# Layer 1 of a two-layer streaming trunk: attention steps and memory turns at fixed product counts inside each main block

## The chip, the cores and the metric

The kernel runs on one core of a Trainium2 chip. The metric is device time in microseconds (us) of one execution. Before the change the median is 1432.3 us of 3 runs (1431.83 to 1434.07).

## What is computed

The program is one inference step of an encoder trunk with two layers, for a prompt of 512 tokens and a sample of 32, which are carried side by side as 544 columns. Layer 0 is a recurrent mixer and is not touched here. Layer 1, cut to what matters:

```python
def diff_layer(x, mk, mv, k_past, v_past, ..., w_out, w_in, ...):
    h = rmsnorm(x, norm_w)
    q, k, v, qm, gate = split(h @ w_in)      # 12 heads of 128 columns each in q, k, v; 4 memory heads in qm; 16 gate blocks
    # per head, q and k have two halves (maps) of 64; blocks of 128 queries, keys masked by chunks of 64
    attn = softmax(q1 @ k1.T / 8) - lam * softmax(q2 @ k2.T / 8)
    o = rmsnorm(attn @ v, subln) * (1 - lam_init)
    y_mem = softmax(qm @ mk.T * 128 ** -0.5) @ mv      # 256 memory rows
    out = concatenate([o, y_mem]) * silu(gate)
    return x + out @ w_out, k, v
```

The prompt's attention is causal by chunks over its own 512 keys; the 32 sample tokens see 128 cached keys and their own 32. Keys and values of both are outputs too.

## The kernel before

Every engine is called through the helper class `Queue`, so line 104 stands at nearly every instruction of the profile; the tiles' names tell them apart. Engines are TensorE (PE, with its weight loads as PEld), VectorE (DVE), ScalarE (ACT), GpSimd (POOL) and SyncE (SP), which issues DMAs.

**Main blocks.** Products of the projection are taken in 32 bits by splitting: a block of 1024 x 128 weights, loaded as two halves `raw`, is split into `whi` (a cast on ACT, two per block) and `wlo` (a subtraction on DVE, two per block); the activations are held as `hh` and `hl`. For each of two column halves of 272 and each of 8 slices of 128 rows, PE does `whi` x `hh`, `whi` x `hl` and `wlo` x `hh` into one bank `ps_g`: 48 products to a block. `proj` and `gemm` (or `steps`, a generator with a stop after each product) emit them, and an evacuation function takes each half out of the bank (`k`, `v`, `qp`/`qs`, the gate `sg`, or the memory query `mq`). `used()` then emits the split of the next block and the load of a later one, in the order of the list from `blocks1`. `whi` and `wlo` have 2 buffers, `raw` 5.

**Banks.** PSUM has 3 banks for `ps_g` (pool `psg`, also `ps_mo`), 2 in `psm` (turnings: `ps_kv`, `ps_kvs`, `ps_ckT`, `ps_aT`, `ps_oT`; memory scores `ps_mm`), 1 in `psx` (`ps_o`, `ps_os`) and 2 in `psc` (scores `ps_s`, and `ps_sc`).

**Layer 1** runs 3 groups of 4 heads. For each head `diff_group` emits the K block, the split of the keys into `kh` and `kz` (with DMAs that fill the other half of `kh`), the Q block, the V block, and then the whole attention of the head in one piece: keys and values turned (`kt`, `vt`, also written out), the sample's keys and values (`vs`), the sample's scores `ps_sc` copied to `ssb`, and for each of four blocks `t` of 128 queries: two maps of scores `ps_s` of (t + 1) x 128 columns, two passes each; mask by memset; maximum `snm` (DVE), exponential `pt` (ACT); `combine` (DVE); t + 1 transposes into `ps_aT`, copied to `aT` (ACT); t + 1 passes of `ps_o`, copied to `ot` (DVE) and squared (`jk`, ACT). After four heads the sample's output (`ps_saT`, `ps_os`, `ps_osT`), the scaling of `ot`, its transposes `ps_oT` and four gate blocks follow. Groups 0 and 1 then have two memory heads each (`mem_head`): a query block and a gate block, with the steps of `mem_steps` emitted behind them. That makes 56 main blocks, and then the output product.

**What sets the order.** In layer 1 the flag `ordered` is off, so a scheduler places each engine's instructions at build time, from the order in which they are emitted, the data they need and the buffers that come free. It may slide a piece of attention between products that are emitted later. At run time each engine's queue is fixed.

## Time and profile before

| | before |
|---|---|
| median of 3 runs | 1432.3 us |
| profiled execution, its own time | 1432.36 us |
| its span in the profile | 1430.4 us |
| PE busy | 1391.5 us (97%) |
| PEld busy | 1309.5 us (92%) |
| DVE, ACT, POOL busy | 64%, 58%, 26% |
| main products `ps_g` of layers 0 and 1, each of three kinds | 1808 |

The span is what the trace covers of the profiled execution; the difference to its own time lies around it. A busy share is an average over stages with different limits. Matmuls are pipelined and overlap, so the busy time of PE includes time in which one of them stands behind another. Weight loads are the second view of the same queue: each matmul has one.

### The profile page before, as it was taken

The numbers are of one execution on the slowest core, as the hardware profiler recorded it, in microseconds if no ns is written. First come the engines' busy times: TensorE is split into PE (matmuls) and PEld (weight loads), VectorE is DVE, ScalarE is ACT, GpSimd is POOL, SyncE is SP. The second block draws the span as 40 slices with busy tenths as digits, with TensorE's granted clock in tenths as the row PEclk, the third lists the DMA queues.
The fourth block names the chain that finished last, engine by engine and source line by source line (L and its number), as shares of the span: only waits on it lengthen the run. The fifth ranks groups of instructions, "written<-read, shape, count | busy, mean of one in ns | idle before, by whom it ended". The sixth has DMA issues, their size and how long they took to land.

```text
span 1430.4 us, 31910 instructions
## 1 busy us (share of the span) xinstructions
PE 1391.5 (97%) x11877; PEld 1309.5 (92%) x11877; DVE 917.7 (64%) x2345; ACT 828.8 (58%) x2282; POOL 375.0 (26%) x838
## 2 busy tenths in 40 slices
PE   8999999999999999999999999999999999999997
PEld 6998899999999998988999999989999989999997
DVE  5776678778777778566734656574465746557443
ACT  5766677777777676656433456554566446565222
POOL 2046557655686557600000220000000001000100
PEclk9999999999999999999999999999999999999999
DMA  7533222333223322432644562323333223332321
GB/s 225 157 106 80 60 58 75 80 83 75 73 66 82 97 68 55 122 93 79 192 142 128 148 188 81 91 79 89 97 90 85 83 75 95 90 103 62 97 80 71
DMA packets 264036, 139.45 MB, mean 97 GB/s; under 512 B 57721, under 2 KB 252802, under 8 KB 263882
## 3 DMA queue, kind: packets, MB, share of 16 engines
q1 hardware_dynamic: 263818, 137.41, 34.1%
q8 instruction: 94, 1.54, 0.5%
q14 instruction: 60, 0.49, 0.1%
q10 hardware_dynamic: 64, 0.02, 0.0%
HBM read 111.12 MB, written 22.91 MB: 94 GB/s over the span
## 4 chain that ended last, share of the span: by engine, by line
PE 82%; DVE 8%; ACT 6%; issue 2%; DMA 1%; SPq 1%; DVEq 0%; ACTq 0%
PE ps_g L104 57%; PE ps_c L104 4%; PE ps_s L104 2%; PE ps_o L104 2%; PE ps_at L104 2%; DVE wlo L104 1%; PE ps_v L104 1%; PE ps_mo L104 1%; PE ps_mm L104 1%; PE ps_aT L104 1%; SPq L104 1%; PE ps_yc L104 1%; PE ps_ss L104 1%; ACT whi L104 1%; PE ps_w L104 1%
## 5 line engine op out<-in xcount | busy, mean ns | idle before, releaser
L104 PE MATMUL ps_g<-hh,wlo 128*128 128x272 f32 x1808 | 538.4, 299 | 2.5 <-DVE wlo L104 2.5
L104 PE MATMUL ps_g<-hh,whi 128*128 128x272 f32 x1808 | 538.6, 299 | 0.2 <-DVE memk L104 0.2
L104 PE MATMUL ps_g<-hl,whi 128*128 128x272 f32 x1808 | 531.8, 295 | 0.6 <-DVE hl L104 0.3
L104 PEld LDWEIGHTS ps_g<-hh,wlo 128*128 128x128 f32 x1808 | 341.7, 189 | 7.5 <-DVE wlo L104 3.6
L104 PEld LDWEIGHTS ps_g<-hh,whi 128*128 128x128 f32 x1808 | 342.4, 190 | 5.2 <-issue 0.5
L104 PEld LDWEIGHTS ps_g<-hl,whi 128*128 128x128 f32 x1808 | 341.8, 189 | 5.0 <-DVE hl L104 1.3
L104 DVE TENSOR_TENSOR wlo<-raw,whi 128x512 fp32r<-128x512 f32 x314 | 216.8, 703 | 191.6 <-ACT whi L104 187.8
L104 ACT CAST whi<-raw 128x512 fp32r<-128x512 f32 x314 | 189.9, 617 | 172.0 <-PE ps_g L104 99.0
L851 POOL TENSOR_TENSOR tm<-u,m 102x84 f32<-102x84 f32 (+23 forms) x341 | 146.6, 430 | 163.2 <-DMA m<-sc 137.4
L853 POOL TENSOR_TENSOR u<-u,tm 102x84 f32<-102x84 f32 (+23 forms) x341 | 147.8, 434 | 26.7
L104 PE MATMUL ps_g<-hi,whi 128*128 128x272 f32 x512 | 148.9, 291 | 0.0
L104 PE MATMUL ps_g<-hi,wlo 128*128 128x272 f32 x512 | 147.8, 289 | 0.8 <-DVE wlo L104 0.8
L104 PE MATMUL ps_g<-lo,whi 128*128 128x272 f32 x512 | 147.6, 288 | 0.0
L1312 POOL TENSOR_TENSOR lo<-og,hi 128x544 fp32r<-128x544 f32 x8 | 13.7, 1708 | 484.0 <-DVE og L104 348.8
L104 PEld LDWEIGHTS ps_g<-hi,wlo 128*128 128x128 f32 x512 | 96.4, 188 | 1.0 <-DVE wlo L104 1.0
L104 PEld LDWEIGHTS ps_g<-lo,whi 128*128 128x128 f32 x512 | 96.4, 188 | 0.0
L104 PEld LDWEIGHTS ps_g<-hi,whi 128*128 128x128 f32 x512 | 96.4, 188 | 0.0
L104 DVE SCALAR_TENSOR_TENSOR SB<-ps_c,dl,sd 64x64 f32<-64x64 f32 x168 | 47.5, 283 | 43.9 <-PE ps_c L104 40.5
L1731 POOL TENSOR_TENSOR hl<-hn,hh 128x544 fp32r<-128x544 f32 x8 | 12.7, 1588 | 212.9 <-ACT hh L104 212.7
L104 ACT COPY sv<-ps_c 64x64 f32<-64x64 f32 x192 | 39.3, 205 | 44.5 <-PE ps_c L104 42.7
L104 ACT ACTIVATE sg<-ps_g 128x272 f32<-128x272 f32 x64 | 25.3, 395 | 64.0 <-PE ps_g L104 62.2
L104 ACT ACTIVATE pt<-ps_s,snm 128x128 f32<-128x128 f32 (+3 forms) x96 | 50.7, 529 | 17.9 <-DVE snm L104 16.9
(388 smaller groups left out, 2599.6 us busy)
## 6 DMA issues: line engine op xcount, KB each, us to landing
raw<-in_rw_in_dram SPq DMA_DIRECT2D x114, 256.0 KB
raw<-in_df_in_dram SPq DMA_DIRECT2D x112, 256.0 KB
raw<-in_w_out_dram SPq DMA_DIRECT2D x64, 256.0 KB
oscr<-sg SPq DMA_DIRECT2D x16, 272.0 KB
lo<-oscr SPq DMA_DIRECT2D x16, 272.0 KB
m<-sc SPq DMA_DIRECT2D x33, 128.0 KB
raw<-in_w_mem_v_dram SPq DMA_DIRECT2D x16, 256.0 KB
kh<-kh SPq DMA_DIRECT2D x24, 136.0 KB
```

The source lines that it names most:

```text
L104: return lambda *a, **k: self.trunk.tie(self, issue(*a, **k))
L851: nc.gpsimd.tensor_tensor(tm[:, :n, :wd], u3[:, :n, kx : kx + 1].to_broadcast(sh), m3[:, kx : kx + 1, kx + 1 :].to_broadcast(sh), ALU.mult)
L853: nc.gpsimd.tensor_tensor(u3[:, :n, kx + 1 :], u3[:, :n, kx + 1 :], tm[:, :n, :wd], ALU.add)
L1312: (self.nc.gpsimd if g % 2 and self.o1 else self.ve).tensor_tensor(lo[:], t, hi[:].bitcast(F32), ALU.subtract)
L1731: nc.gpsimd.tensor_tensor(self.hl[:, k, :], h[:], self.hh[:, k, :].bitcast(F32), ALU.subtract)
```

## The change

Layer 1's emission is rewritten. A new function `block` emits the 48 products of a main block one by one and, before the product whose number a piece carries, calls that piece. The attention of a head becomes a generator (`diff_head`), whose steps are the pieces; so do the group's end (`diff_end`) and the memory turns (`mem_steps`, as before). `groups` holds the table of the counts: a head's steps stand at products 6, 16, 28, 40 of its V block, 10, 20, 30, 40 of the next head's K block and 6, 18, 30, 42 of the next head's Q block. The group's end and the two memory turns of a group are set among the gate and query blocks; the columns in `blocks1` follow the new order of blocks. The sample's scores `ps_sc` are taken from `psm` instead of `psc` and come after the first two prompt scores instead of ahead of them. In layer 1 the memory values `mv`, `cv` are loaded later, in the middle of the turn. The last group's gate blocks have its end among them, and the last head's turning and gating come behind the last gate block.

The core of the diff:

```diff
-    def mem_head(self, i, h, w, cq, cg, p):
-
-        st = {}
-        it = self.mem_steps(st, i, h, p)
...
-    def mem_steps(self, st, i, h, p):
-
-        nc, a, two = self.nc, self.a, 1 + self.ordered
+    def mem_steps(self, st, i, h, p, two):
...
+        def values():
+            mv = p.tile([P, 2, P], F32, tag="mhv", name="mhv", bufs=two)
+            cv = p.tile([P, 2, P], F32, tag="cmv", name="cmv", bufs=two)
+            self.se.dma_start(mv[:], self.mem[i, 1][h][:].rearrange("p (j c) -> p j c", j=2))
+            self.se.dma_start(cv[:], a["cache_mem_v"][i, 0, :, h, :].rearrange("(j p) d -> p j d", p=P))
+            return mv, cv
+
         self.se.dma_start(ct[:], a["cache_mem_k"][i, 0, :, h, :].rearrange("(j p) d -> p j d", p=P))
         self.se.dma_start(mk[:], self.mem[i, 0][h][:])
-        self.se.dma_start(mv[:], self.mem[i, 1][h][:].rearrange("p (j c) -> p j c", j=2))
-        self.se.dma_start(cv[:], a["cache_mem_v"][i, 0, :, h, :].rearrange("(j p) d -> p j d", p=P))
+        if two > 1:
+            mv, cv = values()
...
+        if two == 1:
+            mv, cv = values()
         pT = p.tile([P, 2, T], F32, tag="mpT", name="mpT")
...
-            cols += [3 * MIXW + 512 + h * P for h in range(4 * hg, 4 * hg + 4)]
-            for h in ((0, 1), (2, 3), ())[hg]:
-                cols += [3 * MIXW + h * P, 3 * MIXW + 512 + MIXW + h * P]
+            g = [3 * MIXW + 512 + h * P for h in range(4 * hg, 4 * hg + 4)]
+            if hg < 2:
+                q, m = ([c + h * P for h in (2 * hg, 2 * hg + 1)] for c in (3 * MIXW, 3 * MIXW + 512 + MIXW))
+                g = [g[0], q[0], g[1], g[2], q[1], g[3], m[0], m[1]]
+            cols += g
...
+    def block(self, w, c0, evac, pieces=()):
+
+        pieces, steps = list(pieces), self.steps(self.weights(w, c0), evac)
+        for i in range(6 * KT):
+            while pieces and pieces[0][0] <= i:
+                pieces.pop(0)[1]()
+            next(steps)
+        self.used()
+        for _, fn in pieces:
+            fn()
+
+    def groups(self, w, p, mp, nlam, aside, free):
+
+        late = []
+        for hg in range(3):
+            gr = self.diff_group(hg, p)
+            heads = [self.diff_head(gr, j, p, nlam) for j in range(4)]
+            sgs, fins, prev = [], [], None
+            step = lambda it, *at: [(i, lambda: next(it, None)) for i in at]
+
+            def gate(c0, pieces):
+                self.gates += 1
+                sg, _, evac = self.gate_evac(self.gates)
+                self.block(w, 3 * MIXW + 512 + c0, evac, pieces)
+                return sg
+
+            for j, (parts, it) in enumerate(heads):
+                h = 4 * hg + j
+                before = step(prev, 10, 20, 30, 40) if j else late
+                k, q, v = parts()
+                self.block(w, MIXW + h * P, k, before)
+                if not j and hg == 2:
+                    free()
+                next(it)
+                self.block(w, h * P, q, step(prev, 6, 18, 30, 42) if j else ())
+                if j:
+                    aside()
+                if j == 3 and hg < 2:
+                    mem = [self.mem_turn(1, 2 * hg + i, mp) for i in range(2)]
+                    for _ in range(2):
+                        next(mem[0][1])
+                self.block(w, 2 * MIXW + h * P, v, step(it, 6, 16, 28, 40))
+                prev = it
+            end = self.diff_end(gr, nlam)
+            fin = lambda j, at: (at, lambda: end.send((j, sgs[j])))
+            g0 = 4 * hg * P
+            sgs.append(gate(g0, step(prev, 10, 20, 30, 40)))
+            if hg == 2:
+                sgs.append(gate(g0 + P, step(prev, 6, 18, 30, 42)))
+                aside()
+                sgs.append(gate(g0 + 2 * P, step(end, 2, 10, 18) + [fin(0, 22), fin(1, 36)]))
+                sgs.append(gate(g0 + 3 * P, [fin(2, 16)]))
+                fin(3, 0)[1]()
+                break
+            (st0, m0), (st1, m1) = mem
+            for st, h in ((st0, 2 * hg), (st1, 2 * hg + 1)):
+                st["c"] = h * P
+
+            def query(st):
+                def evac(ps, v):
+                    if not v.start:
+                        st["q"], st["evac"] = self.query_evac(mp)
+                    st["evac"](ps, v)
+                return evac
+
+            self.block(w, 3 * MIXW + st0["c"], query(st0), step(m0, 2) + step(prev, 6, 18, 30, 42))
+            sgs.append(gate(g0 + P, step(end, 8, 20, 36)))
+            sgs.append(gate(g0 + 2 * P, [fin(0, 4)] + step(m0, 14, 14, 28, 28) + step(m1, 30, 30) + [fin(1, 38)]))
+            self.block(w, 3 * MIXW + st1["c"], query(st1), step(m0, 4, 14, 14) + step(m1, 20) + step(m0, 28, 40))
+            sgs.append(gate(g0 + 3 * P, [fin(2, 10)] + step(m1, 22, 22, 36, 36)))
+            sg0 = gate(MIXW + st0["c"], [fin(3, 10)])
+            st0["gate"] = lambda sg0=sg0: sg0
+            sg1 = gate(MIXW + st1["c"], step(m0, 8) + step(m1, 16, 26, 26, 38))
+            st1["gate"] = lambda sg1=sg1: sg1
+            late = step(m1, 8, 22)
...
+        def turned(x, n):
+            t = p.tile([P, 4, P], F32, tag="kt" if n == 4 else "vt", name="kt" if n == 4 else "vt", bufs=n - 3)
+            ps = self.psm.tile([P, 512], F32, tag="m", name="ps_kv")
+            for i in range(4):
+                self.te.transpose(ps[:, i * P : i * P + P], x[:, i * P : i * P + P], self.ident[:])
+            self.ae.copy(t[:], ps[:].rearrange("p (j c) -> p j c", j=4))
+            self.se.dma_start(o[n][0, 0, :, h, :].rearrange("(i p) d -> p i d", p=P), t[:])
+            return t
...
+        def scores(t):
+            n, S = (t + 1) * P, []
+            for m in range(2):
+                ps = self.psc.tile([P, 512], F32, tag="c", name="ps_s")
+                c = slice(t * P, t * P + P)
+                self.te.matmul(ps[:, :n], st["qp"][:, m, c], st["kh"][:, m, :n], start=True, stop=False)
+                self.te.matmul(ps[:, :n], st["qp"][:, m, c], st["kz"][:, m, :n], start=False, stop=True)
+                self.ve.memset(ps[:64, n - 64 : n], -1e30)
+                S.append(ps[:, :n])
+            pt, rs = self.softmax(S, n, p)
+            self.combine(pt, rs, n, nlam)
+            st["pt", t] = pt
+
+        def probs(t):
+            n = (t + 1) * P
+            ps = self.psm.tile([P, 512], F32, tag="m", name="ps_aT")
+            for i in range(t + 1):
+                self.te.transpose(ps[:, i * P : i * P + P], st["pt", t][:, 0, i * P : i * P + P], self.ident[:])
+            st["aT", t] = p.tile([P, 512], F32, tag="aT", name="aT", bufs=2)
+            self.ae.copy(st["aT", t][:, :n], ps[:, :n])
+
+        def weighted(t):
+            aT, ot = st["aT", t], st["ot"]
+            po = self.psx.tile([P, 512], F32, tag="x", name="ps_o")
+            for i in range(t + 1):
+                self.te.matmul(po[:, :P], aT[:, i * P : i * P + P], st["vt"][:, i, :], start=i == 0, stop=i == t)
+            self.ve.tensor_copy(ot[:, t, :], po[:, :P])
+            jk = p.tile([P, P], F32, tag="jk", name="jk", bufs=2)
+            self.ae.activation(jk[:], ot[:, t, :], AF.Square, accum_out=gr["ss"][:, 0, 4 * j + t : 4 * j + t + 1])
...
+        def steps():
+            k, kh, kz = st["k"], st["kh"], st["kz"]
             for m in range(2):
                 hi = kh[rows[m], m, :]
                 self.ae.copy(hi, k[rows[m], :])
                 self.se.dma_start(kh[rows[1 - m], m, :].bitcast(F32), hi.bitcast(F32))
                 self.ve.tensor_tensor(kz[rows[m], m, :], k[rows[m], :], hi.bitcast(F32), ALU.subtract)
+            yield
+            turned(k, 4)
             if j == 0:
                 ps = self.psm.tile([P, 512], F32, tag="m", name="ps_ckT")
                 for i in range(4):
+                    self.te.transpose(ps[:, i * P : i * P + P], gr["ck"][:, i, :], self.ident[:])
+                self.ae.copy(gr["ckT"][:, :, :P], ps[:].rearrange("p (j c) -> p j c", j=4))
+            self.ae.copy(gr["ckT"][:, j, P:], k[:, TP:])
+            yield
+            scores(0)
+            yield
+            scores(1)
+            yield
+            ps = self.psm.tile([P, 512], F32, tag="m", name="ps_sc")
+            self.te.matmul(ps[:, : P + TS], st["qs"][:], gr["ckT"][:, j, :], start=True, stop=True)
             for m in range(2):
+                self.ae.copy(gr["ssb"][32 * j : 32 * j + 32, m, :], ps[m * TS : m * TS + TS, : P + TS])
+            probs(0)
+            yield
+            st["vt"] = turned(st["v"], 5)
+            ps = self.psm.tile([P, 512], F32, tag="m", name="ps_kvs")
+            for i, x in enumerate((k, st["v"])):
+                self.te.transpose(ps[:, i * P : i * P + P], x[:, T - P :], self.ident[:])
+            self.ae.copy(gr["vs"][:, :, j, :], ps[P - TS :, :256].rearrange("p (j c) -> p j c", j=2))
+            st["ot"] = p.tile([P, 4, P], F32, tag="ot", name="ot", bufs=4)
+            gr["on"].append(st["ot"])
+            yield
+            scores(2)
+            probs(1)
+            yield
+            weighted(0)
+            yield
+            scores(3)
+            yield
+            probs(2)
+            weighted(1)
+            yield
+            weighted(2)
+            yield
+            probs(3)
+            yield
+            weighted(3)
+            yield
+
+        return parts, steps()
...
+    def diff_end(self, gr, nlam):
...
+        ask = yield
+        while True:
+            j, sg = ask
+            on = gr["on"][j]
             for t in range(4):
+                self.ve.tensor_scalar(on[:, t, :], on[:, t, :], ss[:, 2, 4 * j + t : 4 * j + t + 1], None, ALU.mult)
             ps = self.psm.tile([P, 512], F32, tag="m", name="ps_oT")
             for t in range(4):
+                self.te.transpose(ps[:, t * P : t * P + P], on[:, t, :], self.ident[:])
             g = self.dest(4 * hg + j, sg)
             self.ve.scalar_tensor_tensor(g[:, :TP], ps[:], self.subs, sg[:, :TP], ALU.mult, ALU.mult)
             self.ve.tensor_tensor(g[:, TP:], oT[:, 32 * j : 32 * j + 32], sg[:, TP:], ALU.mult)
+            ask = yield
...
```

How the scheduler then orders the engines, at three places. First PE, at the second head of the first group. `ps_g` are main products, `ps_s` the prompt's scores (two passes for each of two maps). Before, in the K block that follows its V block, from behind the first map of the first scores:

```order
L104 MATMUL ps_g<-hh,whi 128x272
L104 MATMUL ps_g<-hl,whi 128x272
L104 MATMUL ps_g<-hh,wlo 128x272
L104 MATMUL ps_g<-hh,whi 128x272
L104 MATMUL ps_g<-hl,whi 128x272
L104 MATMUL ps_g<-hh,wlo 128x272
L104 MATMUL ps_s<-kh,qp 128x128
L104 MATMUL ps_s<-kz_12302,qp 128x128
L104 MATMUL ps_s<-kh,qp 128x256
L104 MATMUL ps_s<-kz_12302,qp 128x256
```

After the change, from product 16 of the head's V block:

```order
L104 MATMUL ps_g<-hh,whi 128x272
L104 MATMUL ps_s<-kh,qp 128x128
L104 MATMUL ps_s<-kz_12302,qp 128x128
L104 MATMUL ps_s<-kh,qp 128x128
L104 MATMUL ps_s<-kz_12302,qp 128x128
L104 MATMUL ps_g<-hl,whi 128x272
L104 MATMUL ps_g<-hh,wlo 128x272
L104 MATMUL ps_g<-hh,whi 128x272
L104 MATMUL ps_g<-hl,whi 128x272
L104 MATMUL ps_g<-hh,wlo 128x272
L104 MATMUL ps_g<-hh,whi 128x272
L104 MATMUL ps_g<-hl,whi 128x272
```

The second map of the first scores stood products behind the first map, and the second scores (256 columns) followed it directly. Now both maps stand together inside the V block, and the second scores come after twelve products, at count 28.

Second ACT, at the same head, around the first exponentials. `qp` and `qs` are the evacuations of the Q block, `v` of the V block, `kt` is the copy of the turned keys, `vt` and `vs` of the values, `ssb` of the sample's scores, `pt` the exponentials. Before, from the evacuation of the V block:

```order
L104 COPY v<-ps_g 128x272
L104 CAST whi<-raw 128x512
L104 COPY v<-ps_g 128x272
L104 CAST whi<-raw 128x512
L104 COPY kt<-ps_kv 128x512
L104 COPY vt<-ps_kv 128x512
L104 COPY ssb<-ps_sc 32x160
L104 COPY vs<-ps_kvs 32x2x128
L104 COPY ssb<-ps_sc 32x160
L104 ACTIVATE pt,srs<-ps_s,snm 128x128 x2
L104 ACTIVATE pt,srs<-ps_s,snm 128x256
L104 COPY aT<-ps_aT 128x128
```

After, from the Q block's evacuation:

```order
L104 CAST whi<-raw 128x512
L104 ACTIVATE qp<-ps_g 64x272
L104 CAST whi<-raw 128x512
L104 COPY kt<-ps_kv 128x512
L104 ACTIVATE qs_12298<-ps_g 64x32
L104 ACTIVATE qp<-ps_g 64x272
L104 ACTIVATE qs_12298<-ps_g 64x32
L104 ACTIVATE pt,srs<-ps_s,snm 128x128 x2
L104 COPY v<-ps_g 128x272
L104 ACTIVATE pt,srs<-ps_s,snm 128x256 x2
L104 COPY ssb<-ps_sc 32x160 x2
L104 COPY aT<-ps_aT 128x128
```

The exponentials of the first scores stood behind five copies of turnings and sample scores; now they stand behind `qp` and `qs` of the Q block, and the copies of `ps_sc` come after the second exponentials.

Third ACT, at the end of the next K block, where the head's last steps and the split of the keys meet. `kh` is the cast of the keys, `aT` the copy of turned probabilities, `jk` the squares. Before:

```order
L104 CAST whi<-raw 128x512
L104 ACTIVATE pt,srs<-ps_s,snm 128x512
L104 ACTIVATE jk,oss<-ot 128x128
L104 CAST whi<-raw 128x512
L104 COPY aT<-ps_aT 128x384
L104 CAST kh<-k 64x544 x2
L104 COPY ckT<-k 128x32
L104 ACTIVATE qp<-ps_g 64x272
L104 ACTIVATE jk,oss<-ot 128x128
L104 COPY aT<-ps_aT 128x512
```

And after:

```order
L104 COPY k<-ps_g 128x272
L104 CAST whi<-raw 128x512
L104 ACTIVATE pt,srs<-ps_s,snm 128x512
L104 CAST whi<-raw 128x512
L104 CAST kh<-k 64x544 x2
L104 COPY aT<-ps_aT 128x384
L104 ACTIVATE jk,oss<-ot 128x128
```

Both casts of `kh` stood behind the 384-wide `aT`; now they stand ahead of it, and the weight casts `whi` of the next block ahead of both.

More of the change, by code (lines that the diff above doesn't have):

```diff
@@ L1197, in softmax @@
         return pt, rs
-    def mem_head(self, i, h, w, cq, cg, p):
-        st = {}
-        it = self.mem_steps(st, i, h, p)
-        for _ in range(3):
-            next(it)
-        st["q"], evac = self.query_evac(p)
-        self.proj(w, cq + h * P, evac)
-        for _ in range(9):
-            next(it)
-        sg = self.gate(w, cg + h * P)
-        st["gate"] = lambda: sg
-        for _ in it:
-            pass
     def query_evac(self, p, bufs=1):
@@ L1783, in layer1, with aside, free @@
                         nc.gpsimd.memset(t[r, m, :].bitcast(F32), 0.0)
[L1784 to L1793 removed]
+                pe, early = [], iter(order[:MADE])
+                def aside():
+                    if pe:
+                        made.update({g: self.gated(g, *self.fetch(pe[0], g)) for g in islice(early, 2)})
+                def free():
+                    m1.close()
+                    pe.append(self.pool("wo1e", 1, ctx=ctx, side="right"))
+                self.groups(w, p, mp, nlam, aside, free)
             p = self.pool("wo1", 1, ctx=ctx)
```

129 lines of the change are left out of this document (41 added, 88 removed).

## The prediction

> **What bounds the kernel now.** I read the page's busy shares first, then a table of stretches of layer 1, then who waits for whom, and last the instructions of one head in order of time.
>
> ```profile
> span 1430.4 us, 31910 instructions
> PE 1391.5 (97%) x11877; PEld 1309.5 (92%) x11877; DVE 917.7 (64%) x2345; ACT 828.8 (58%) x2282; POOL 375.0 (26%) x838
> ```
>
> TensorE (PE) sets the end, so only its lost time counts. The profiled execution took 1432.36 us, 1.96 beyond its span and 0.06 above the median of 1432.3; differences against its trace are taken off the median. The change reorders one stage. The order of instructions is the same up to its first attention piece (at about 848 us) and again in the last output product, so I look from 836 to 1318 us. A main block is 48 products into `ps_g`; most rows below run from the start of one block to that of the next. Columns: stretch, its length, then busy us of PE, PEld (weight loads), DVE, ACT, POOL, each with its count; then PE clock, DMA share, GB/s.
>
> ```profile
> 836.00:1318.00 482.00, 477.19 (x3574) 446.29 (x3573) 286.97 (x843) 270.49 (x794) 5.31 (x3) 1.00 0.32 90
> 1010.66:1016.69 6.03, 6.03 (x50) 6.03 (x49) 3.61 (x6) 3.62 (x8) 0.00 (x0) 1.00 0.48 131
> 877.24:888.69 11.45, 11.10 (x76) 9.72 (x76) 8.19 (x32) 7.76 (x29) 0.00 (x0) 1.00 0.33 93
> 888.69:897.14 8.45, 8.45 (x71) 8.38 (x70) 5.41 (x12) 5.42 (x16) 0.00 (x0) 1.00 0.37 97
> 897.14:904.70 7.56, 7.56 (x63) 7.33 (x61) 2.96 (x5) 4.09 (x11) 0.00 (x0) 1.00 0.25 70
> 943.37:953.62 10.25, 10.24 (x89) 9.04 (x88) 6.81 (x28) 5.25 (x18) 0.00 (x0) 1.00 0.28 79
> 953.62:962.08 8.46, 8.46 (x68) 7.93 (x66) 7.26 (x30) 2.47 (x6) 0.00 (x0) 1.00 0.21 63
> 968.33:976.27 7.94, 7.92 (x59) 7.39 (x58) 3.49 (x7) 3.50 (x8) 0.00 (x0) 1.00 0.29 85
> 976.27:986.52 10.25, 10.25 (x73) 8.98 (x71) 6.00 (x14) 5.60 (x17) 0.00 (x0) 1.00 0.23 66
> ```
>
> A block with nothing beside it takes 6.03 us, 0.126 a product, and its weight loads have no gap. The next three rows are one head's whole cycle, 27.46 us: in the first of them weight loads fill 9.72 of 11.45 although PE reads 11.10 busy. The busy time of overlapping matmuls hides a loss there. Where it comes from:
>
> ```profile
> PEld ps_o L104 <- ACT aT L104: 5.7, 27, 0.3
> PEld ps_s L104 <- ACT ssb L104: 4.9, 12, 0.5
> ```
> ```profile
> 877.98 0.11 DVE L104 MEMSET ps_s<- 64x64 f32 x1
> 878.92 0.28 ACT L104 COPY ssb<-ps_sc 32x160 f32<-32x160 f32 x1
> 879.25 0.19 PEld L104 LDWEIGHTS ps_s<-kh,qp 128*128 128x128 f32 x1 [0.36 <-ACT ssb L104]
> 880.42 0.58 DVE L104 TENSOR_REDUCE snm<-ps_s 128x1 f32<-128x128 f32 x2
> 880.71 0.37 ACT L104 ACTIVATE pt<-ps_s,snm 128x128 f32<-128x128 f32 x1 [1.02 <-DVE snm L104]
> ```
>
> The first list is of PE's waits, with total us, times and longest: scores (`ps_s`) wait once per head for the copy that empties `ps_sc`, which holds one of the two score banks, and `ps_o` for the copy of `aT`. The second shows it at one head. Scores, memset, reduction, exponential and turning follow each other with 2 to 13 products between, fewer than the chain takes.
>
> **How much is lost.** I set each head against the spacing of the same matmuls where nothing waits. From the chain of work:
>
> ```profile
> 848.16 0.66 PE ps_kv L104 x6
> 890.68 0.67 PE ps_o L104 x6
> 951.07 0.75 PE ps_os L104 x16
> 984.43 2.08 PE ps_mo L104 x8
> ```
> ```profile
> 854.12 0.28 PE L104 MATMUL ps_s<-kh,qp 128*128 128x256 f32 x1
> 854.24 0.29 PE L104 MATMUL ps_s<-kz,qp 128*128 128x256 f32 x1
> 879.26 0.33 PE L104 MATMUL ps_s<-kh,qp 128*128 128x128 f32 x1
> 879.42 0.28 PE L104 MATMUL ps_s<-kz,qp 128*128 128x128 f32 x1
> 883.70 0.33 PE L104 MATMUL ps_s<-kh,qp 128*128 128x384 f32 x1
> 883.87 0.34 PE L104 MATMUL ps_s<-kz,qp 128*128 128x384 f32 x1
> 884.67 0.39 PE L104 MATMUL ps_s<-kh,qp 128*128 128x512 f32 x1
> 884.90 0.39 PE L104 MATMUL ps_s<-kz,qp 128*128 128x512 f32 x1
> ```
>
> Start to start, a score pass takes 0.16, 0.12, 0.17 and 0.23 us at 128, 256, 384 and 512 columns. One head is three blocks (3 x 6.03 = 18.09), 20 transposes at 0.11 (2.20), 20 passes of `ps_o` at 0.112 (2.23), four score passes of each size (2.72) and two of `ps_sc` at some 0.14 (0.28): 25.52. It took 27.46, so 1.94 is lost, 23.3 over 12 heads. At a group's end the first block holds 9 transposes, 14 `ps_o` and the 0.75 of `ps_os`: 6.03 + 0.99 + 1.57 + 0.75 = 9.34 of 10.25; the next holds 17 transposes: 7.90 of 8.46. That is 1.5 lost, 4.4 over three groups. Of a memory turn's two blocks I take the first as free of waits, which makes a pass of `ps_mm` (7.94 - 6.03)/8 = 0.24; the second is 6.03 + 0.48 + 12 x 0.11 + 2.08 = 9.91 of 10.25, so 0.34, 1.4 over four turns. Together 29.1 us: that is the most the change can win.
>
> The Trainium skill's front page (Trainium Kernel Development and Optimization, Performance Expectations) says matmul busy time is a bad measure and that of the weight loads a good one. By matmul busy time this stage could win 482.00 - 477.19 = 4.8 us, by weight loads 35.7. The spacings side with the weight loads, and their 29.1 stands without the page.
>
> **The change part by part.** On every engine the number of instructions by kind is the same, so nothing is removed or added, only moved.
>
> *The scores.* `ps_sc` moves from the score banks to the other pool, so the wait for `ssb` (4.9 in the list) cannot come back in that form. Pieces now stand 10 to 19 products apart, 1.26 to 2.39 us. What is late next? I followed both in-order queues for one head, with these durations:
>
> ```profile
> 877.15 0.59 ACT L104 COPY kt<-ps_kv 128x512 f32<-128x512 f32 x1
> 887.81 0.69 ACT L104 ACTIVATE pt<-ps_s,snm 128x512 f32<-128x512 f32 x1 [0.18 <-DVE snm L104]
> 888.88 0.39 ACT L104 COPY k<-ps_g 128x272 f32<-128x272 f32 x1
> 889.17 0.62 ACT L104 CAST whi<-raw 128x512 fp32r<-128x512 f32 x1
> 889.77 0.48 ACT L104 COPY aT<-ps_aT 128x384 f32<-128x384 f32 x1
> 890.66 1.31 ACT L104 CAST kh<-k 64x544 fp32r<-64x544 f32 x2
> 897.86 0.39 ACT L104 ACTIVATE qp<-ps_g 64x272 fp32r<-64x272 f32 x1
> 899.06 0.19 ACT L104 ACTIVATE qs<-ps_g 64x32 f32<-64x32 f32 x1 [0.29 <-DVE qp L104]
> 898.60 0.43 DVE L104 SCALAR_TENSOR_TENSOR qp<-ps_g,qp 64x272 fp32r<-64x272 f32 x1
> ```
>
> (a) First to second scores: four passes (0.64) and 12 products (1.51), 2.15 us. Alone, the chain is ready in time: two passes 0.32, memset 0.11, reduction 0.29, exponential 0.37, 1.1 for one map; the second bank 0.36 later, needed 0.24 later. But ahead of those exponentials ACT has, from the query block's end, `whi`, `qp`, `whi`, `kt`, `qs`, `qp`, DVE's `qp` and `qs`: 0.62 + 0.39 + 0.62 + 0.59 + 0.19 + 0.39 + 0.43 + 0.19 = 3.4 us, while the first scores start 2.45 after it (16 products, 4 transposes). So the exponentials start about 1.3 after the scores instead of 0.7, and the second scores are on time or up to 0.4 late. I take 0.2.
> (b) Third `ps_o`: it needs the 384-wide `aT`, which on ACT follows the second `k` copy, `whi`, an exponential, `whi` and both `kh`: 0.39 + 0.62 + 0.69 + 0.62 + 1.31 + 0.48 = 4.1 us from the key block's end, and some 0.15 until `k` can start. On PE that point is 6 products, 3 transposes, 4 passes and 19 products away: 3.9. It is 0.4 late. After a group's last head a gate block follows, without `kh`, so it isn't late there.
> (c) Third to fourth scores have 20 products, two transposes and two passes (2.9 us) against two reductions and exponentials (about 2.3); the turnings have 24 or more products. I cost them at nothing; the products between are the cover. If the queues ran a `whi` (0.62) later, both would be late.
>
> So 9 heads lose 0.6 and 3 lose 0.2: 6.0. Beside that I leave each head 0.3, as the two uncrowded blocks of a head now lose in all: 3.6. *Group ends*: the first two get 9 to 48 products between pieces (0.3 left each), the third still has its transposes one by one behind the scaling (1.0): 1.6. *Memory turns*: two are now woven into each other; no row shows that, so between 0 and twice 1.4; I take 1.2. Left: 6.0 + 3.6 + 1.6 + 1.2 = 12.4. *Moved transfers*: the later value loads of a memory turn have over 100 products (13 us) before use; `kt` and `vt` writes now stand apart in SP's queue, each ahead of weight loads that run more than a block ahead (6 us). I cost both at nothing; a load late by one ACT copy would be 0.6. *The end*: the last four transposes now follow the last gate block, yet the output product needs that head only after 168 of its products (21 us). Nothing.
>
> Gain 29.1 - 12.4 = 16.7; 1432.3 - 16.7 = **1415.6**.
>
> **The rivals.**
> *All of it goes* (0.18): (a) and (b) are met by chance and the leftovers with them; 29.1 at most, some 24 likely: 1408, down to 1403. For it: PE's pieces are the same and uncrowded blocks lose only 0.1 each.
> *The waits move* (0.12): (a) 0.7 late because a `whi` gets in front, (b) 1.2. Then a head loses 1.9 as now, and the time is 1432, within 0.2%. Had the scheduler not followed the counts it would be the same; the rows of the order show that it did.
> *Slower* (0.10): fixed places leave PE nothing to slide forward. If ACT, which is busy some 19 of 25.5 us in a head, runs behind all through, four joints per head ((a), (b) and both of (c)) are late together. From 0.5 each the head loses as much as now; at 0.75, a `whi` and a handover, 12 x 4 x 0.75 = 36 and 6.4 besides: 42 against 29, **1445**. Against it: (c) shows 0.6 to spare, and ACT has waits of its own for DVE, as the `qs` row shows, that shrink.
> The Trainium skill has a rule that backs it (TensorE: Matmul & The Clock Gate, its specification table and Part 2): ACT and DVE are strict first-in-first-out, and PE pulls only weight loads ahead, never matmuls. The `qs` row, 0.29 idle with other work queued, agrees.
>
> **How the numbers follow.** The forecast has 0.60: 1408 to 1425, its joints between half and twice as late. The range takes in the full gain and leaves out the slower case and part of the unchanged one: 1403 to 1430. About 0.2% (3 us) is what a measurement of this kernel tells from no change. Faster 0.78 (the forecast and the full gain), same 0.12, slower 0.10.
>
> **What would show it.** Right: a head's cycle near 26.3 us, no wait of `ps_s` for `ssb`, waits of `ps_o` for `aT` once per head near 0.4, and a stage of some 465 us instead of 482 in which weight loads are idle for some 19 us instead of 35.7. Wrong: `ps_s` waiting for `pt` four times a head, `ps_g` waiting for `whi` or `wlo` (weights late), or a longer stretch after the stage.

## The result and the profile after

The changed kernel takes 1410.43 us in the median of 4 runs (1409.44 to 1411.84) against 1432.3 (1431.83 to 1434.07): a ratio of 0.9846, 95% interval 0.9829 to 0.9863. That is 21.9 us less, where 16.7 was forecast, and inside the range of 1403 to 1430.

The page of the changed kernel, its span and its busy time:

```profile
span 1407.5 us, 31863 instructions
PE 1368.6 (97%) x11877; PEld 1304.7 (93%) x11877; DVE 932.4 (66%) x2345; ACT 823.9 (59%) x2282; POOL 374.7 (27%) x838
```

PE's share is the same 97%, although the kernel is 1.5% shorter: its busy time shrank with the span. So the stretches tell it, not the shares. I measure a *stage* here, from the start of the third main block, the first with attention work in it, to the first output product. In the profiles of different kernels the blocks ahead of it start up to 3.5 us apart, so pieces of a us or two are compared by the stage and not by the whole time. Columns are as in the prediction: stretch, its length, busy us of PE, PEld, DVE, ACT and POOL with counts, clock, DMA share, GB/s. Before, the stage:

```profile
841.70:1317.77 476.07, 471.26 (x3527) 440.36 (x3526) 284.24 (x839) 267.41 (x786) 5.31 (x3) 1.00 0.31 89
```

After, the stage, then its first V block, and then the V block of the second head, the K block that follows it and the Q block after that, which carry that head's attention:

```profile
841.25:1295.23 453.98, 450.05 (x3527) 437.35 (x3526) 298.17 (x839) 262.42 (x787) 4.83 (x3) 1.00 0.33 93
841.25:851.23 9.98, 8.74 (x69) 8.32 (x68) 7.02 (x24) 6.66 (x22) 0.00 (x0) 1.00 0.76 209
869.27:877.08 7.81, 7.81 (x66) 7.81 (x64) 5.42 (x19) 5.69 (x21) 0.00 (x0) 1.00 0.35 101
877.08:885.83 8.75, 8.75 (x68) 8.54 (x67) 5.94 (x17) 4.80 (x15) 0.00 (x0) 1.00 0.32 92
885.83:895.17 9.34, 9.07 (x75) 8.85 (x74) 6.24 (x14) 6.47 (x19) 0.00 (x0) 1.00 0.32 88
```

The whole gain lies in the stage: 476.07 - 453.98 = 22.1 us. A head's three blocks take 7.81 + 8.75 + 9.34 = 25.90 us instead of 27.46. In the V block weight loads fill the whole 7.81; in the Q block they are still idle for 9.34 - 8.85 = 0.49. PE's matmul time left 476.07 - 471.26 = 4.8 us idle before and leaves 3.9 now; weight loads left 35.7 and leave 16.6. A reader of matmul busy time would have said that 4.8 us is all there was to win. The Trainium skill's page named for this in the prediction (Trainium Kernel Development and Optimization, Performance Expectations) agrees with these rows.

What weight loads wait for in the stage now (us in total, times, longest):

```profile
PEld ps_o L104 <- ACT aT L104: 4.2, 9, 0.5
PEld ps_mo L104 <- issue: 3.8, 16, 0.2
PEld ps_s L104 <- DVE qp L104: 0.9, 1, 0.9
PEld ps_ckT L104 <- DMA ck<-in_cache_k_dram: 0.8, 1, 0.8
```

The waits of scores for `ssb` and for `pt` are gone; `ps_o` waits for `aT` nine times, once for each head but the last of a group.

### The profile page after: what moved, and what is told of

The parts are those of the page before. It is cut to its first block, busy times and chain, and to the rows that moved or that the text cites. A ratio compares the mean times of both kernels' runs of the same rounds, so it can differ in the third digit from the quotient of the medians.

```text
span 1407.5 us, 31863 instructions
## 1 busy us (share of the span) xinstructions
PE 1368.6 (97%) x11877; PEld 1304.7 (93%) x11877; DVE 932.4 (66%) x2345; ACT 823.9 (59%) x2282; POOL 374.7 (27%) x838
## 4 chain that ended last, share of the span: by engine, by line
PE 78%; DVE 9%; ACT 8%; issue 2%; DMA 1%; SPq 1%; DVEq 0%; ACTq 0%
PE ps_g L104 54%; PE ps_c L104 4%; PE ps_at L104 2%; PE ps_o L104 2%; ACT pt L104 2%; PE ps_s L104 2%; DVE wlo L104 2%; PE ps_v L104 1%; ACT whi L104 1%; PE ps_mm L104 1%; PE ps_mo L104 1%; PE ps_ss L104 1%; PE ps_yc L104 1%; PE ps_w L104 1%; ACT kh L104 1%
```

## The experiments

Each run was timed together with the kernel before, which then took 1433.1 to 1434.0 us instead of the 1432.3 above. Medians from different runs are therefore compared only to a microsecond or two; the ratios and the lengths of the stage carry the argument.

### Undoing the counts alone

```diff
-                self.block(w, 2 * MIXW + h * P, v, step(it, 6, 16, 28, 40))
+                self.block(w, 2 * MIXW + h * P, v)
                 prev = it
+                for _ in it:
+                    pass
```

> The changed kernel with all steps of a head emitted in one piece behind its V block, in the same order and with the same pools (ps_sc in the pool of the turnings); the group's end and the memory turns keep their counts. PE's order then has the steps crowded again into the block behind V. Theory (the counts bring the gain: each link of the chain gets as many products as it takes): a head's cycle goes back from 25.9 to about 27.2 us, 12 heads 16 us, 1410.4 + 16 = 1426 (1421 to 1431). Rival (the order of the steps and the pools bring it, the places do not matter since the scheduler slides pieces anyway): 1410 to 1414, cycle below 26.3.

Measured: 1426.92 us, ratio to before 0.9951 (0.9937 to 0.9965). The K block behind the second head's V block, and the first waits of the stage:

```profile
877.74:889.29 11.55, 11.00 (x80) 10.16 (x80) 8.47 (x32) 7.72 (x26) 0.00 (x0) 1.00 0.33 92
```
```profile
PEld ps_s L104 <- ACT pt L104: 7.5, 12, 0.8
```

The head's cycle is 27.22 us, the block is crowded as in the kernel before (11.45 there), and weight loads are idle for 1.4 us of it. The wait is not the old one for `ssb`; it is for the exponentials, which come last as soon as `ssb` is out of the way. So the places bring 16.2 of the stage's 22.1 us (470.19 against 453.98), and the scheduler by itself does not spread the steps. Of the 5.9 us that stay won without them, 3.7 lie in the group ends and memory turns, which keep their counts here, and 2.2 in the heads, from the order of the steps and the pools; these two were not taken apart further.

### The bank of the sample's scores, alone in both directions

In the kernel before, moved:

```diff
-            ps = self.psc.tile([P, 512], F32, tag="c", name="ps_sc")
+            ps = self.psm.tile([P, 512], F32, tag="m", name="ps_sc")
```

> The kernel before with one edit: the sample's scores ps_sc take their bank from the pool of the turnings instead of the score banks. Theory (too few products stand between the steps of a head, whichever wait is named last): the wait of ps_s for ssb (4.9 us in the list of before) goes, but the exponentials then come last; gain 0 to 2 us, 1431 (1430 to 1432.5). Rival (the bank was the cause): the 4.9 us go, 1427.4, a head's cycle 27.05.

Measured: 1433.01 us, ratio 0.9994 (0.9985 to 1.0003); the stage is 475.17 us, 0.9 less. The crowded block of the second head and the waits of the stage:

```profile
879.50:890.80 11.30, 11.11 (x78) 9.99 (x78) 8.82 (x34) 8.59 (x29) 0.00 (x0) 1.00 0.33 94
```
```profile
PEld ps_o L104 <- ACT aT L104: 6.2, 29, 0.3
PEld ps_s L104 <- ACT pt L104: 4.7, 15, 0.4
PEld ps_kv L104 <- ACT v L104: 3.9, 12, 0.3
```

A wait of 4.9 us is gone and the block is 0.15 shorter, and the interval of the ratio takes in no change at all; the waits for `pt` (3.3 before) and `v` (2.7) have grown. The list names only what came last at each place; in a crowded block the next link is right behind.

In the changed kernel, the same line put back to `psc`:

> The changed kernel with the sample's scores back in the score banks. Theory (at product 40 the bank of the second scores' first map has just been read, 0.1 us late; the rest of the gain comes from the counts): at most 0.2 us a head, 1410.4 + 2 = 1412 (1410 to 1413). Rival (the bank is what the change won): a wait of ps_s or ps_sc of 0.4 a head or more, 1415 and up.

Measured in a single run: 1413.22 us, just above the range given; the stage is 456.76 us, 2.8 more. The V block of the second head:

```profile
870.82:878.85 8.03, 8.03 (x65) 7.82 (x64) 5.61 (x20) 5.71 (x21) 0.00 (x0) 1.00 0.35 100
```

It takes 8.03 instead of 7.81. With the counts the bank is worth 0.22 us in nine heads, while the first head of the second and third group takes what it took (8.23 against 8.21). Another 0.6 of the 2.8 lies in the first V block of all, whose length varies (see below). Without the counts the 0.9 us of the stage come to 0.08 a head.

### The heads alone

The heads keep their counts; the group's end, the gating and the memory turns are emitted whole, between blocks:

```diff
-            sgs.append(gate(g0 + P, step(end, 8, 20, 36)))
...
+            sgs.append(gate(g0 + P, step(prev, 6, 18, 30, 42)))
+            for _ in range(3):
+                next(end)
...
+                self.block(w, 3 * MIXW + c, evac)
+                for _ in range(9):
+                    next(m)
```

> The changed kernel with the heads' steps at their counts, but the group's end, its gating and the memory turns emitted in one piece each between blocks, as before, and the columns' order of before. Theory: the heads keep their cycle of 25.9 us; of the blocks behind them the lost time is again that of before (2.8 a group against 1.2, and 1.7 against 0.6 in the last): 1410.4 + 4.4 = 1414.8 (1412.5 to 1416.5). Rival (the interleaving of the memory turns brings most of it): above 1420.

Measured: 1413.96 us, ratio 0.986 (0.9846 to 0.9873); the stage is 456.03 us, 2.05 more than with all of the change, and a head's cycle is the same 25.9. So the heads bring 20 of the 22.1 us, and the group ends and memory turns 2, half of what I had expected. The two blocks of a group's end, and a memory turn's two blocks:

```profile
938.80:947.82 9.02, 9.02 (x77) 8.98 (x76) 5.97 (x17) 5.65 (x21) 0.00 (x0) 1.00 0.21 60
947.82:956.39 8.57, 8.57 (x79) 7.61 (x76) 8.10 (x40) 3.08 (x11) 0.00 (x0) 1.00 0.30 93
963.34:971.26 7.92, 7.90 (x59) 7.37 (x57) 3.49 (x7) 3.06 (x8) 0.00 (x0) 1.00 0.29 84
971.26:981.50 10.24, 10.24 (x72) 8.97 (x71) 6.00 (x14) 5.61 (x17) 0.00 (x0) 1.00 0.22 66
```

The memory blocks are those of before (7.94 and 10.25). What I had missed is the first block of the group's end: it profits from the counts of the last head's steps, without any of the interleaving behind it (9.02 us here, 10.25 before).

### How much a joint holds

Second scores set earlier, group by group:

```diff
-                self.block(w, 2 * MIXW + h * P, v, step(it, 6, 16, 28, 40))
+                self.block(w, 2 * MIXW + h * P, v, step(it, 6, 16, (28, 24, 20)[hg], 40))
```

> The changed kernel with the second scores emitted at product 28 of the V block in the first group, at 24 in the second and at 20 in the last; in PE's order the first map then stands at 28, 24 and 22, the second at 28, 25 and 25. Theory (the second scores come just on time at 28: their banks are free some 1.5 and 1.95 us behind the start of the first scores): V blocks lose 0.02, 0.25 and 0.4 us. Rival (there is time to spare at this joint): all three lose nothing.

Measured in a single run of 1414.31 us, the V block of each group's second head:

```profile
870.54:878.34 7.80, 7.80 (x66) 7.80 (x65) 5.42 (x19) 5.68 (x21) 0.00 (x0) 1.00 0.35 101
1037.38:1045.57 8.19, 8.13 (x66) 7.89 (x64) 5.88 (x20) 5.93 (x21) 0.00 (x0) 1.00 0.35 98
1205.57:1213.91 8.34, 8.04 (x65) 7.82 (x64) 5.80 (x20) 6.05 (x21) 0.00 (x0) 1.00 0.33 94
```

Nothing, 0.39 and 0.54 us are lost. There is hardly any time to spare at this joint: 12 products are just about what the chain takes, and 8 to 9 are too few. The loss is larger than expected by some 0.15 in both.

Then unused work added at two joints, on one engine each:

```diff
-            turned(k, 4)
+            kt = turned(k, 4)
+            if gr["hg"] < 2:
+                more = (self.ae.copy, self.ve.tensor_copy)[gr["hg"]]
+                for i in range(2):
+                    more(self.junk[:], kt[:, i, :])
...
             k, kh, kz = st["k"], st["kh"], st["kz"]
+            if gr["hg"] == 2:
+                for i in range(2):
+                    self.ae.copy(self.junk[:], k[:, T - P:])
```

> The changed kernel with work added that nothing uses, two copies of 128 x 128 a head (about 0.56 us): in the first group on ACT behind the copy of kt, ahead of the first exponentials; in the second the same on DVE, ahead of the mask and the maxima of the first scores; in the last on ACT beside the casts of kh, ahead of the 384-wide aT. Theory, read from the trace of the changed kernel (ahead of the first exponentials ACT waits 0.52 and 0.26 us for DVE, while DVE works without a gap; ahead of aT ACT works without a gap): V blocks of the first group stay at 7.80 (up to 0.1 more), V blocks of the second take 0.5 more (8.3), Q blocks of the last group's heads 0.56 more (9.9). Rival, the sum of the prediction, which ran the first joint over ACT's queue: V blocks of the first group take 0.5 more and those of the second none.

Measured in a single run of 1412.68 us, a V block of the first group, a V block of the second and a Q block of the last:

```profile
871.98:879.79 7.81, 7.81 (x65) 7.81 (x64) 5.42 (x19) 6.29 (x23) 0.00 (x0) 1.00 0.36 101
1038.50:1046.70 8.20, 8.20 (x66) 7.89 (x64) 5.78 (x21) 5.69 (x21) 0.00 (x0) 1.00 0.34 98
1222.80:1232.02 9.22, 9.08 (x75) 8.85 (x74) 6.24 (x14) 6.86 (x21) 0.00 (x0) 1.00 0.34 89
```

ACT carries 0.60 us more in the first row, ahead of the first exponentials, and the block is not longer; DVE's extra costs 0.40. The first joint hangs on DVE's queue, not on ACT's. The third row goes against the expectation: 9.22 instead of 9.9, less even than the 9.34 without the extra work. PE's order explains it: with two more copies on ACT the scheduler put the third `ps_o` behind product 29 of the Q block instead of 25. The piece moved with the work, so this group says nothing on the price of ACT's work there.

### The last joint: the third output of a head

In the changed kernel's trace, ACT's instructions ahead of the 384-wide `aT`, and PE's weight load that waits for it (start, us, what, in brackets the idle time before it and what ended it):

```profile
887.77 0.62 ACT L104 CAST whi<-raw 128x512 fp32r<-128x512 f32 x1
888.28 1.32 ACT L104 CAST kh<-k 64x544 fp32r<-64x544 f32 x2
889.63 0.48 ACT L104 COPY aT<-ps_aT 128x384 f32<-128x384 f32 x1
890.16 0.74 PEld L104 LDWEIGHTS ps_o<-vt,aT 128*128 128x128 f32 x6 [0.49 <-ACT aT L104]
```

First PE's side: the piece set later.

```diff
-                self.block(w, h * P, q, step(prev, 6, 18, 30, 42) if j else ())
+                self.block(w, h * P, q, step(prev, 6, 30, 32, 44) if j else ())
```

> The changed kernel with one table row altered: the third output piece of a head stands at product 30 of the next Q block instead of 18, the turning behind it at 32, the fourth output at 44. Theory (the remaining loss of a head is PE arriving 0.5 us ahead of the 384-wide aT, which ACT copies behind two weight casts and two casts of kh): 5 products later is 0.63 us later, so the 0.5 goes in 8 heads and the Q block takes 8.82 us instead of 9.34; time 1410.4 - 4.2 = 1406.2 (1405 to 1407.5). Rival (ACT is behind all through, so the wait moves to the next piece, the fourth output): Q block stays near 9.3, time 1410.

Measured: 1411.58 us, ratio 0.9843 (0.983 to 0.9856); the stage is 453.17 us, 0.8 less than with the change. The second head's Q block, and behind it PE's fourth output and ACT's instructions ahead of its `aT`:

```profile
889.27:898.50 9.23, 9.08 (x76) 8.86 (x75) 6.25 (x14) 6.41 (x18) 0.00 (x0) 1.00 0.33 89
```
```profile
895.50 0.40 ACT L104 ACTIVATE qp<-ps_g 64x272 fp32r<-64x272 f32 x1 [1.14 <-DVE qp L104]
896.35 0.59 ACT L104 COPY aT<-ps_aT 128x512 f32<-128x512 f32 x1
896.99 0.97 PEld L104 LDWEIGHTS ps_o<-vt,aT 128*128 128x128 f32 x8 [0.37 <-ACT aT L104]
```

The rival's outcome: 0.11 us in the Q block, not 0.5. The third output no longer waits, but the fourth waits 0.37 for its own copy. Not because ACT is behind all through: in the new order that copy stands behind a `qp`, for which ACT was idle 1.14 us, waiting for DVE.

Then ACT's side: the casts set behind the copy.

```diff
-                next(it)
-                self.block(w, h * P, q, step(prev, 6, 18, 30, 42) if j else ())
+                if not j:
+                    next(it)
+                self.block(w, h * P, q, step(prev, 6) + step(it, 7) + step(prev, 18, 30, 42) if j else ())
```

> The changed kernel with the casts of kh emitted behind the turning of the 384-wide probabilities (product 7 of the Q block) instead of ahead of the Q block; ACT then copies aT ahead of both casts, and PE's third output stands at product 18 instead of 25. Theory: the copy ends 1.3 us sooner (about 888.8 instead of 890.1 in the second head), PE asks for it 0.9 us sooner than now; of the 0.53 a head 0.3 is left, 8 heads: time 1410.4 - 1.9 = 1408.5 (1407.5 to 1409.5). Rival one (the kh casts are not what the copy waits for): no gain, or slower by 0.9 a head, 1417. Rival two (keys now late for the next scores): a wait of ps_s for kh in each V block.

Measured: 1408.18 us, ratio 0.9819 (0.9806 to 0.9833); the stage is 450.27 us, 3.7 less than with the change. The Q block:

```profile
889.13:898.03 8.90, 8.90 (x75) 8.87 (x74) 6.33 (x14) 6.47 (x19) 0.00 (x0) 1.00 0.36 92
```

It takes 8.90 instead of 9.34, no `ps_o` is left in the list of waits, and no `ps_s` waits for `kh`. The casts were what the copy waited for, and the third output stands at its count of 18 again. The expectation left 0.3 a head; 0.08 is left (8.90 against 8.82 by the prediction's spacings).

### The first V block

It takes 9.98 us, where the second group's takes 8.21. DVE's and PE's instructions in it, in the changed kernel:

```profile
842.17 0.29 DVE L104 TENSOR_TENSOR lp<-lam 128x128 f32<-128x128 f32 x1 [3.33 <-DMA lam<-in_df_lk_dram]
```
```profile
843.12 0.66 PE L104 MATMUL ps_ckT<-ident,ck 128*128 128x128 f32 x4 [0.52 <-DMA ck<-in_cache_k_dram]
845.76 0.30 PE L104 MATMUL ps_s<-kh,qp 128*128 128x128 f32 x1 [0.72 <-DMA kh<-kh]
```

DVE stands 3.33 us at the arithmetic on lambda, with `qp` queued behind it. The kernel before has the same order there (DVE stands 3.74 us), but its first scores come 6.5 us later (852.23 instead of 845.76). So `ck` was loaded first and the arithmetic emitted later:

```diff
+                gr0 = self.diff_group(0, p)
                 lam = p.tile([P, 4, 64], F32, name="lam")
...
+                first = [(8, lams)] if not h else []
+                self.block(w, 2 * MIXW + h * P, v, step(it, 6) + first + step(it, 16, 28, 40))
```

> The changed kernel with the first group's cached keys loaded ahead of lambda's four vectors, and the arithmetic on lambda emitted at product 8 of the first V block instead of ahead of all. In the trace of the changed kernel the first V block loses 1.76 us, the other eleven 0.02: DVE stands 3.3 us at lp, waiting for the load of lam, with qp queued behind it, and PE waits for ck and for the first scores' operands. Theory: the 1.76 goes, 1410.4 - 1.7 = 1408.7, and the first V block takes 8.2 us. Rival (the load of kh is late by itself, since it is queued behind weight loads): 0.7 stays, 1409.4.

Measured: 1410.34 us, ratio 0.9842 (0.9826 to 0.9859); the stage is 0.6 us shorter. The first V block, and an instruction of ACT in it:

```profile
842.16:851.59 9.43, 8.91 (x70) 8.43 (x68) 6.15 (x22) 6.27 (x21) 0.00 (x0) 1.00 0.72 183
```
```profile
843.81 0.20 ACT L104 ACTIVATE ls<-ls 128x2 f32<-128x2 f32 x1 [3.12 <-DVE ls L104]
```

Neither expectation: 1.2 us stay, and not because of `kh`, for which PE now waits 0.2. The scheduler placed lambda's exponential on ACT ahead of the weight casts, so that ACT stood 3.12 us where DVE had stood. The gain itself is small against what this block varies: in the runs above that leave its steps as they are, it takes 10.1 to 10.4 us, against 9.98 with the change.

### Both mends together

The casts behind `aT`, and lambda worked out in layer 0's last part: its vectors laid down the partitions and summed by one product with ones:

```diff
+        for j, n in enumerate(("df_lq1", "df_lk1", "df_lq2", "df_lk2")):
+            self.se.dma_start(lam[:, j : j + 1], self.a[n].rearrange("o d -> d o"))
...
             rs = self.token_rms((sums,), p)
+            self.ve.tensor_tensor(lp[:], lam[:, 0:4:2], lam[:, 1:4:2], ALU.mult)
+            ps = self.psm.tile([P, 512], F32, tag="m", name="ps_lam")
+            self.te.matmul(ps[:, :2], self.ones[:64, :], lp[:], start=True, stop=True)
+            self.ae.activation(ls[:, :2], ps[:, :2], AF.Exp)
...
+                gr0 = self.diff_group(0, p)
```

> The changed kernel with the casts of kh behind the 384-wide aT, as in the run that showed it, and the first V block's load waits taken away: the first group's cached keys are loaded ahead of the layer's other small loads, and lambda is loaded and worked out in layer 0's last part (its vectors laid down the partitions and summed by one product with ones), so that neither DVE nor ACT stands at it. Theory (3.7 us of the stage from kh as measured, and 1.7 to 2.0 of the first V block): 1410.4 - 3.7 - 1.8 = 1404.9 (1403.5 to 1406.5), the first V block 8.2 us. Rival (the load of kh is late by itself in the first head): 0.7 to 1.2 stays in that block, 1406. Rival two (the moved lambda holds up a queue in layer 0): the stage is as short, but starts later.

Measured: 1406.77 us (1406.0 to 1409.49), ratio 0.9816 (0.9802 to 0.9829). The stage, the first V block and the second head's Q block:

```profile
843.74:1291.95 448.21, 447.77 (x3527) 437.31 (x3526) 297.39 (x834) 261.76 (x785) 4.84 (x3) 1.00 0.33 93
843.74:851.93 8.19, 8.19 (x69) 8.19 (x68) 5.62 (x20) 6.29 (x20) 0.00 (x0) 1.00 0.55 155
886.10:895.00 8.90, 8.90 (x75) 8.87 (x74) 6.34 (x14) 6.47 (x19) 0.00 (x0) 1.00 0.34 92
```

The first V block now takes what the others take, so the load of `kh` was not late by itself. The stage is 448.21 us, 5.8 less than with the change and 27.9 less than before. The median is 1.9 above the 1404.9 expected and just outside the range given with it, although the stage did what was expected of it (5.5). The second rival is why: the stage is as short, but starts later. From one and the same product of layer 0 (at 698.09 us with the change) to the stage it takes 144.9 us here and 143.1 to 143.3 in all the other kernels, before and after included. Two places make up 1.5 of this 1.7 us. First come the loads of lambda in SP's queue and, 18 us on, a wait of PE for a weight split:

```profile
694.52 0.47 SPq L104 DMA_DIRECT2D lam<-in_df_lq_dram  x1
712.75 0.39 PE L104 MATMUL ps_g<-hi,wlo 128*128 128x272 f32 x1 [0.82 <-DVE wlo L104]
```

The four loads stand ahead of those that layer 0 itself needs, which are issued 2.4 us later behind the store ahead of them than with the change, and 1.1 us is lost at that wait. Then the product with ones (`ps_lam`, at 802.61) costs PE 0.4. That the loads cause the wait is read from the order of the queues; it was not tried by itself.

## Why the prediction came out as it did

**What bounds the kernel** held. Only PE's lost time counted, the loss lay in the crowded blocks, and the view of weight loads was the right one. Of the signs named, `ps_o` waits for `aT` as forecast, while the head's cycle (25.90 us against 26.3) and the idle time of weight loads (16.6 against some 19) fell further.

**The budget of 29.1 us** was short by about 2.4. I had taken 0.16 us for a score pass of 128 columns from the two starts at 879.26 and 879.42. In the changed kernel the four passes start like this:

```profile
871.72 0.22 PE L104 MATMUL ps_s<-kh,qp 128*128 128x128 f32 x1
871.79 0.27 PE L104 MATMUL ps_s<-kz,qp 128*128 128x128 f32 x1
871.90 0.27 PE L104 MATMUL ps_s<-kh,qp 128*128 128x128 f32 x1
872.01 0.28 PE L104 MATMUL ps_s<-kz,qp 128*128 128x128 f32 x1
```

That is 0.11 or less. The first pass before stood right behind a wait (0.36 for `ssb`), so my spacing "where nothing waits" seems to have had part of a wait in it: 4 x 0.05 for each of 12 heads.

**The group ends and memory turns** (lost 5.8, left 1.6 + 1.2, so a gain of 3.0) came out at 3.0: from the end of a group's first gate block, the one right behind its last V block, to the start of the next group's first V block (in the last group to the output product), before and after differ by 1.2, 1.2 and 0.7 us. Of that, 1.7 is the interleaving: with the heads alone these stretches are 0.78, 0.75 and 0.18 longer than with all of the change. The other 1.3 are the last heads' own counts. So the size was met, but in part by luck: as the expectation for the heads alone shows, I had put all of it down to the interleaving.

**The heads** are where the forecast was off: 13.7 expected (23.3 less 6.0 and 3.6), 19.0 found (22.1 less the 3.0 of the group ends and memory turns, before rounding). By its joints:

- *(a), first to second scores*, forecast 0.2 late. It is on time: V blocks lose 0.03 (7.81 against 6.03 + 4 x 0.11 for `ps_kv`, 4 x 0.11 and 4 x 0.12 for the scores, 0.28 and 0.11 for `ps_sc` and `ps_aT`), and the second scores start at 873.68, 1.96 behind the first. The exponentials start 1.16 us behind the first scores, where I had written 1.3. That it is so near is luck: my own sum gives 1.0 (3.4 less 2.45), and the queue that I added up was the wrong one:

```profile
872.41 0.11 DVE L104 MEMSET ps_s<- 64x64 f32 x1
```
```profile
872.44 0.19 ACT L104 ACTIVATE qs<-ps_g 64x32 f32<-64x32 f32 x1 [0.52 <-DVE qp L104]
872.88 0.37 ACT L104 ACTIVATE pt<-ps_s,snm 128x128 f32<-128x128 f32 x1 [0.26 <-DVE snm L104]
```

 ACT is idle twice, waiting for DVE, and the added work showed the same (none for ACT, 0.40 for DVE). The spacing run shows that the joint is on time with next to nothing to spare. So the lateness was mis-sized by 0.2, inside the 0 to 0.4 that I had allowed, and the chain that sets it was misread: it runs over DVE.
- *(b), the third output*, forecast 0.4 in 9 heads, from the casts of `kh` ahead of `aT`. It was 0.49 in weight loads (9.34 - 6.03 - 7 x 0.11 - 18 x 0.112 = 0.52 by the prediction's spacings), nine times and not at a group's last head. Mechanism, place and cause stand: the casts set behind the copy take it away.
- *(c)*, cost at nothing, was nothing: K blocks take 8.75 in every head.
- *The leftover* of 0.3 a head is the term that failed most. It was carried over from the blocks that lose 0.1 each today, as if those losses were a property of PE. Most of them must have been waits like the others, since with a place for each step they went: outside (b), a head loses about 0.05.
- *What was not in the sum at all*: 1.76 us in the first V block, where the head's steps, now earlier, met loads that had been early enough before. I had followed the queues of a head in the steady run, and this one starts the layer.

So 2.4 (spacing), 12 x 0.25 (leftover) and 12 x 0.2 (a) were gained over the forecast, 9 x 0.1 (b) and 1.76 lost: 5.1 of the 5.3 us that the heads were off.

**The rivals.** "All of it goes" (1408) is nearer than the forecast (1415.6), and half for its reason: (a) was met and the leftovers went, but (b) was not met. "The waits move" and "slower" needed ACT to be behind at every joint. By the three rows of a head in the section on the result it is busy 17.0 of 25.9 us, less than the 19 of 25.5 in the prediction (whose own three rows give 17.3 of 27.46), and at the first joint its 0.78 us of waiting took in 0.60 of added work at no cost. By the list of waits it was late ahead of the 384-wide `aT` and hardly anywhere else. The run with the third output at 30 shows, though, how a moved piece turns one wait into the next, and that was the shape of that rival.

## What to carry to other kernels

Where a long chain of small steps shares TensorE with a stream of products that wait for nothing, give each step a place in the stream; reading which wait is named last and mending that one alone won 0.9 of the stage's 22.1 us here, and no time that could be told from nothing. To size such a change, take the spacing of each kind of matmul from a place where the instruction ahead did not wait, set every block against it, and follow the chain over each engine's queue, not only the busiest-looking one. Then look at the first turn of the loop by itself, since its loads and its setup arithmetic were timed by the old order. Where such a load is moved ahead, look also at what it then holds up: here 1.7 us of what the mends won were lost in the layer before.

## What was not expected of the hardware and the scheduler

A small load was slow in a queue that also held weight loads of 256 KB: the last of lambda's four vectors, 32 KB, was issued at 836.95 and the work on it began at 842.17, 5.2 us later. DVE stood 3.33 us at it, and the evacuation `qp` behind it waited too. Whether the loads around it or its own form, one row copied to 128 partitions, made it slow was not tried. And a count in the table is not always the place: the scheduler set the third output, given at product 18, at 25, and with more work on ACT at 29, yet PE still arrived 0.49 and 0.37 us too early. Why it sets the piece so, and why that falls short, was not tried.
